# A hybrid trunk layer whose instruction order comes from the framework's timeline model instead of its functional simulator's clock

## The chip, the cores and the metric

The kernel runs on one core of one Trainium2 chip. A core has five engines with an instruction queue each: TensorE (PE; its weight loads are listed apart as PEld), VectorE (DVE), ScalarE (ACT), GpSimd (POOL) and SyncE (SP, which here only issues transfers). The metric is the device time of one execution in microseconds. Each engine takes its own instructions in the order in which they stand in its queue, and one that waits holds up all behind it.

## The reference

One layer of a decoder trunk, for one sequence of 512 tokens and a model width of 1024, in float32:

```python
h = rms_norm(x, norm1_g[i])
proj = h @ w_in[i]          # S5 input | q | k | v | RWKV-7 inputs | 3 groups of gates
y_a = s5_mixer(...)         # complex diagonal SSM, scan over time, GLU
y_b = diff_attention(...)   # 4 heads, QK norm, two softmaxes subtracted
y_c = rwkv7_mixer(...)      # 8 heads of 64: a state updated token by token
branch_out = jnp.einsum('blnc,ncd->blnd', branches, w_branch[i])
merged = jnp.sum(gates * branch_out, axis=2)
x = x + (merged @ w_out[i])
h2 = rms_norm(x, norm2_g[i])
gu = h2 @ w_ffn_in[i]
x = x + ((silu(gu[..., :D_FF]) * gu[..., D_FF:]) @ w_ffn_out[i])
```

Of the three mixers, the one that matters most below is RWKV-7's scan, in which each token's state needs the one before:

```python
sa = jnp.einsum('bhvk,bhk->bhv', state, a_t)
state = state * w_t + sa * b_t + v_t * k_t
y_t = jnp.einsum('bhvk,bhk->bhv', state, r_t)
```

## The kernel before

Activations lie transposed, 128 channels on the partitions and 512 tokens along the free axis. There are two kinds of work for TensorE.

**Dense matmuls.** Each projection (class `Dense`) keeps float32 accuracy with three reduced-precision matmuls for each block of 128 rows: high part times high part (L1296), high times low (L1297), low times high (L1298), 512 columns each. `tokens` (L1267 to L1285, for attention's k and v) does the same with 256 columns (L1280 to L1282). A weight block comes by a transfer, ScalarE makes its high part (L1225) and VectorE its low part (L1226). The dense matmuls of the mixers depend on nothing but `h` and their weights, so they can stand nearly anywhere.

**Small matmuls.** The mixers are long chains of small float32 matmuls, each of which TensorE does in two passes (an "x2" in the rows). RWKV-7 works on four pairs of heads, and each pair goes through these stages:

- prep (`_prep`, L360): two low-rank matmuls (L366, L371), and on VectorE the norm of `k` with a reciprocal root in a dozen tiny rows (`rsqrt`, L227 to L243; L239, L240 and L242 are its loop; L398 and L263 follow), whose sums are made by L258 and spread by L265; near its end VectorE's L421 writes `kb`.
- local (`_local`, L437): eight transposes of `kb` (L446), then the products within a chunk of 64 tokens (L464, L475).
- inverse (`_inverse`, L495): through DRAM and back (L503, L504), fifteen steps of two VectorE rows each (L513, L515), and through DRAM again (L522 to L527).
- join (`_join`, L535): six groups of small matmuls (L552 to L589), with a copy by ScalarE or VectorE between each and the next.
- chain (`chain`, L595): eight steps, one for each chunk. A step is L619 on TensorE (the state with this chunk's keys, `pT`), L621 on VectorE, L626 on TensorE (`pU`), L627 on ScalarE, then L631, L634 and L636 on TensorE, and L646 on VectorE, which makes the next state Z; ScalarE copies the outputs (L638) and scales Z (L650). L619 of the next step needs L646's Z.

S5's parameters, phases and quarters multiply complex tables on VectorE (`cmul`, L706 to L711) and have small matmuls of their own (L915, L931, L952, L963, L1001, L1005). Attention's are L1156, L1157, L1179 and L1184.

**What sets the order.** The program is written once, in the order that a string names (`ORDER`, line 43): P, T, I, J and C are prep, local, inverse, join and chain of the pair named by the digit, R the inputs of RWKV, S, H, U, Q and Y the pieces of S5, X, K and A those of attention, G one or more gates. The chains come as C0, C1, C3 and C2:

```python
ORDER = ("L R00 G1 R01 R02 P0 T0 I0 R10 R12 S R11 U0 P1 R20 R22 R21 T1 H0 G1 J0 U1 I1 J1 C0 P2 T2 F0 U3 U2 Q0 C1 G3 Q1 G2 H1 I2 Q2 R31 "
         "F1 R32 R30 P3 T3 J2 G1 I3 J3 C3 G1 Q3 X0 K0 A0 G2 Y0 C2 Y1 Y2 Y3 F3 X1 K1 G1 A1 F2 X2 K2 O0 O2 O3 G2 A2 X3 K3 G3 O1 A3")
```

This is not yet the order on the engines. The framework takes the whole program, walks it with a clock that says when each engine would be free and each operand ready, and lets instructions of later steps go ahead of those that are not ready; program order decides between several that are. The queues that come out of it are fixed when the kernel is built, and the chip only follows them. Buffers are chosen by the program before that, so a later user of a buffer waits for its readers in any order. After the mixers come the merge by gates, the output projection, SwiGLU (class `SevenProducts`) and the last projection, nearly all dense.

## Time and profile before

| | |
|---|---|
| median of 3 runs | 1011.51 us (1007.04 to 1014.56) |
| the profiled execution | 1011.71 us, its span 1009.9 us |
| mean granted clock of TensorE | 0.986 |
| busy: TensorE, VectorE, ScalarE, GpSimd | 968.3, 753.6, 473.2, 143.8 us |
| mixers | 0 to 537 us |
| merge, output projection, SwiGLU, last projection | 537 to 1009.9 us |

The page gives, for one execution, the busy time of each engine, the span in 40 slices, the transfers, the chain of work that ended last, and the costliest groups of instructions. The trace behind it gives the start and length of each instruction. A matmul's recorded length is from its start until its end leaves the pipeline, so two that follow each other overlap in the records. [...]

### The profile page before, as it was taken

What the parts mean: (1) busy time and instruction counts of PE and PEld (TensorE: products, weight loads), DVE (VectorE), ACT (ScalarE), POOL (GpSimd) and SP (SyncE); (2) the same over time, 40 slices, a digit from 0 to 9 for tenths busy, and PEclk for the clock granted to TensorE, in tenths of its full rate; (3) what the DMA queues carried; (4) which work ended last, traced back from release to release, by engine and by line L of the source; (5) the groups of instructions that cost most, each with busy time, mean ns of one, the idle gap of its engine ahead of it and who ended that gap; (6) DMA issues with size and microseconds to landing.
All of it is one profiled execution on the core that took longest, in us unless ns stands there. A gap on an engine that the chain in (4) does not pass through costs nothing. (4 is left out here: it accounts for less than half of the span.)

```text
span 1009.9 us, 17897 instructions
## 1 busy us (share of the span) xinstructions
PE 968.3 (96%) x6416; PEld 825.5 (82%) x6416; DVE 753.6 (75%) x1941; ACT 473.2 (47%) x978; POOL 143.8 (14%) x176
## 2 busy tenths in 40 slices
PE   6989999989999999999999899989999999999998
PEld 5767777767779787878886788889999999988886
DVE  7999666889996789977866555779989998843232
ACT  6634324424333566545455224556666666632220
POOL 3022020531420010000000332012211211000000
PEclk9999799999999999999999999989999999999999
DMA  7324252221333234252458864466667676344441
GB/s 242 116 75 112 66 121 75 74 55 53 101 106 75 79 95 126 84 157 74 152 166 282 241 206 151 143 153 159 152 160 183 143 153 169 73 149 122 136 131 37
DMA packets 105593, 129.95 MB, mean 129 GB/s; under 512 B 45376, under 2 KB 47296, under 8 KB 105504
## 3 DMA queue, kind: packets, MB, share of 16 engines
q1 hardware_dynamic: 99168, 117.28, 38.6%
q0 software_dynamic: 6336, 11.54, 7.4%
q8 instruction: 50, 0.82, 0.3%
q14 instruction: 39, 0.32, 0.1%
HBM read 109.90 MB, written 18.88 MB: 128 GB/s over the span
## 5 line engine op out<-in xcount | busy, mean ns | idle before, releaser
L1225 ACT CAST wh<-wr 128x512 fp32r<-128x512 f32 x198 | 120.3, 611 | 210.6 <-PE bank L1297 169.1
L1226 DVE TENSOR_TENSOR wl<-wr,wh 128x512 fp32r<-128x512 f32 x198 | 135.9, 689 | 81.1 <-ACT wh L1225 80.4
L1296 PE MATMUL bank<-act_hi,wh 128*128 128x512 f32 x360 | 149.3, 415 | 8.0 <-ACT wh L1225 5.9
L1297 PE MATMUL bank<-act_lo,wh 128*128 128x512 f32 x360 | 148.4, 412 | 2.0 <-DVE act_lo L253 2.0
L1298 PE MATMUL bank<-act_hi,wl 128*128 128x512 f32 x360 | 148.8, 413 | 0.0
L1385 PE MATMUL bank<-act_hi,wh 128*128 128x256 f32 x352 | 99.7, 283 | 3.4 <-ACT wh L249 3.4
L1385 PE MATMUL bank<-act_hi,wl 128*128 128x256 f32 x352 | 99.4, 283 | 0.2
L1385 PE MATMUL bank<-act_lo,wh 128*128 128x256 f32 x352 | 99.0, 282 | 0.0
L1385 PE MATMUL bank<-sp_t,wh 128*128 128x256 f32 x528 | 96.5, 283 | 0.0
L1296 PEld LDWEIGHTS bank<-act_hi,wh 128*128 128x128 f32 x360 | 69.6, 193 | 22.1 <-ACT wh L1225 5.9
L1297 PEld LDWEIGHTS bank<-act_lo,wh 128*128 128x128 f32 x360 | 69.4, 193 | 16.4 <-DVE act_lo L253 3.4
L1385 PEld LDWEIGHTS bank<-sp_t,wh 128*128 128x128 f32 x528 | 82.1, 191 | 0.0
L1298 PEld LDWEIGHTS bank<-act_hi,wl 128*128 128x128 f32 x360 | 69.4, 193 | 14.2 <-issue 0.6
L1385 PE MATMUL bank<-sp_t,wl 128*128 128x256 f32 x264 | 74.7, 283 | 0.0
L1385 PEld LDWEIGHTS bank<-act_hi,wh 128*128 128x128 f32 x352 | 67.7, 192 | 3.9 <-ACT wh L249 3.8
L1296 PE MATMUL bank<-act,wh 128*128 128x512 f32 x176 | 68.5, 389 | 0.0
L1297 PE MATMUL bank<-act,wh 128*128 128x512 f32 x176 | 68.5, 389 | 0.0
L1298 PE MATMUL bank<-act,wl 128*128 128x512 f32 x176 | 68.5, 389 | 0.0
L1385 PEld LDWEIGHTS bank<-act_hi,wl 128*128 128x128 f32 x352 | 67.4, 192 | 0.8 <-DVE wl L250 0.8
L1385 PEld LDWEIGHTS bank<-act_lo,wh 128*128 128x128 f32 x352 | 67.4, 192 | 0.0
L249 ACT CAST wh<-ar 128x512 fp32r<-128x512 f32 x79 | 48.2, 622 | 27.6 <-DMA ar<-in_w_ffn_in 13.3
L250 DVE TENSOR_TENSOR wl<-ar,wh 128x512 fp32r<-128x512 f32 x79 | 53.5, 687 | 9.1 <-ACT wh L249 7.0
(492 smaller groups left out, 2218.0 us busy)
## 6 DMA issues: line engine op xcount, KB each, us to landing
wr<-in_w_in SPq DMA_DIRECT2D x88, 256.0 KB, 3.0
ar<-in_w_ffn_in SPq DMA_DIRECT2D x46, 256.0 KB, 3.2
wr<-in_w_ffn_out SPq DMA_DIRECT2D x40, 256.0 KB, 2.7
gate<-ar SPq DMA_DIRECT2D x24, 256.0 KB, 2.5
wr<-in_w_branch SPq DMA_DIRECT2D x24, 256.0 KB, 3.3
ar<-gate SPq DMA_DIRECT2D x24, 256.0 KB, 3.4
ar<-in_w_ffn_in POOLq DMA_DIRECT2D x22, 256.0 KB, 3.9
sp_raw<-in_w_ffn_in SPq DMA_DIRECT2D x21, 256.0 KB, 3.2
```

Source lines behind the costliest of these rows:

```text
L249: nc.scalar.copy(hi, src)
L250: nc.vector.tensor_tensor(lo, src, hi.bitcast(F32), ALU.subtract)
L1225: nc.scalar.copy(wh, raw)
L1226: nc.vector.tensor_tensor(wl, raw, wh.bitcast(F32), ALU.subtract)
L1296: nc.tensor.matmul(ps, wh[:, j], hi(k), start=k == 0, stop=False)
L1297: nc.tensor.matmul(ps, wh[:, j], lo(k), start=False, stop=False)
L1298: nc.tensor.matmul(ps, wl[:, j], hi(k), start=False, stop=k == nk - 1)
L1385: nc.tensor.matmul(ps, w[x][:, c], b(y, j), start=first and j == js[0] and n == 0, stop=last and j == js[-1] and n == 2, skip_group_check= ...
```

## The change

```diff
@@ def kernel(**inputs) @@
-    with tile.TileContext(nc) as tc:
+    with tile.TileContext(nc, schedule_with_timeline_sim=True) as tc:
         trunk_kernel(tc, args, out)
```

The clock by which the framework walks the program is taken from another model: a timeline model of the engines in place of its functional simulator. The instructions stay the same, with the same operands and the same dependencies; their order in the queues differs. Of the 5542 matmuls of the kernel 3411 stand elsewhere in TensorE's queue, on VectorE 1691 of 1943 rows, on ScalarE 744 of 946, on GpSimd 88 of 180, and of SyncE's issues 294 of 474; nearly all of them belong to the mixers, and SwiGLU's order hardly changes. TensorE goes from dense to small matmuls or back 328 times in the order before and 198 times in the new one.

The first place is TensorE's queue in the chain of pair 3 (C3), about one and a half steps of it. Here `rw_T` is the tile `ts` that L621 writes and `rw_Z` the state Z. Before:

```order
L626 MATMUL bank_87<-rw_T_224,ar_9_77 128x128
L1296 MATMUL bank_83<-act_hi,wh_143 128x512
L1297 MATMUL bank_83<-act_lo,wh_143 128x512
L631 MATMUL bank_85<-ar_4_72,ar_1_69 128x128
L634 MATMUL bank_86<-ar_5_73,ar_4_72 128x128
L636 MATMUL bank_86<-ar_6_74,rw_Z_221 128x128
L1179 MATMUL bank_89<-ident,ar_6_74 128x128 x2
L1298 MATMUL bank_83<-act_hi,wl_144 128x512
L619 MATMUL bank_87<-rw_Z_222,ar_6_74 128x128
L1296 MATMUL bank_83<-act_hi,wh_148 128x512
```

And in the changed kernel:

```order
L626 MATMUL bank_87<-rw_T_224,ar_9_77 128x128
L631 MATMUL bank_85<-ar_4_72,ar_1_69 128x128
L634 MATMUL bank_86<-ar_5_73,ar_4_72 128x128
L636 MATMUL bank_86<-ar_6_74,rw_Z_221 128x128
L619 MATMUL bank_87<-rw_Z_222,ar_6_74 128x128
L626 MATMUL bank_85<-rw_T_223,ar_9_77 128x128
```

Attention's L1179 and the dense L1296 to L1298 no longer stand between the chain's matmuls. Counted over the whole queue (two matmuls of 256 columns as one of 512), 632 dense matmuls stand ahead of the first L446 of pair 3 before and 816 in the new order; from there to the fourth step of pair 2's chain the count rises to 807 before, and stays at 816 in the new order.

The second place is TensorE's queue at the end of the first chain (C0), where the prep of pair 2 (P2) begins: the last L619 and L626 of the chain, and the prep's L366 and L371. Before:

```order
L619 MATMUL bank_86<-rw_Z_221,ar_1_69 128x128
L1298 MATMUL bank_84<-act_hi,wl_140 128x512
L1296 MATMUL bank_84<-act_hi,wh_137 128x512
L1297 MATMUL bank_84<-act_lo,wh_137 128x512
L1298 MATMUL bank_84<-act_hi,wl_140 128x512
L626 MATMUL bank_87<-rw_T_224,ar_8_76 128x128
L366 MATMUL bank_86<-ar_10_78,rw_wl 128x512
L1296 MATMUL bank_84<-act_hi,wh_137 128x512
L634 MATMUL bank_85<-ar_3_71,ar_2_70 128x128
L636 MATMUL bank_85<-ar_1_69,rw_Z_221 128x128
L371 MATMUL bank_87<-ar_10_78,rw_wl 128x512
L1297 MATMUL bank_84<-act_lo,wh_137 128x512
```

And in the changed kernel:

```order
L619 MATMUL bank_86<-rw_Z_221,ar_1_69 128x128
L1005 MATMUL bank_89<-ar_12_80,ar_13_81 128x64 x2
L1001 MATMUL bank_89<-ar_6_74,ar_13_81 128x128
L1001 MATMUL bank_89<-ar_12_80,ar_14_82 128x128
L1005 MATMUL bank_89<-ar_12_80,ar_13_81 128x64 x2
L626 MATMUL bank_87<-rw_T_224,ar_8_76 128x128
L366 MATMUL bank_86<-ar_10_78,rw_wl 128x512
L634 MATMUL bank_85<-ar_3_71,ar_2_70 128x128
L636 MATMUL bank_85<-ar_1_69,rw_Z_221 128x128
L371 MATMUL bank_87<-ar_10_78,rw_wl 128x512
L915 MATMUL bank_90<-ident,ar_13_81 128x128 x4
L931 MATMUL bank_89<-ar_13_81,s5cb_s_1788 32x128 x4
```

Small matmuls of S5 stand where dense ones stood. From the fifth step of this chain to the first of the second (C1) four dense matmuls are left; the dense ones stand ahead of the fifth step (548 are ahead of it in the new order, 424 before) and in the second chain (744 ahead of its eighth step, 542 before).

The third place is VectorE's queue in the prep of pair 0 (P0), the end of the reciprocal root: L239, L240, L242 and L398 write its tiles `rqt_rw` and `ri_rw`, and the rows between them are `cmul` of S5. Before, with the small tables of S5's parameters:

```order
L239 TENSOR_TENSOR rqt_rw_487<-rqy_rw_494 128x8
L710 TENSOR_TENSOR s_tm_786<-s_pi_781,s_pr_780 128x16
L706 TENSOR_TENSOR s_pr_780<-s_pr_780 128x32
L240 TENSOR_TENSOR rqt_rw_487<-rqt_rw_487,rqx_rw_481 128x8
L711 TENSOR_TENSOR s_pi_781<-s_pi_781,s_tm_786 128x16
L806 TENSOR_TENSOR s_nr_823<-s_em_98_742,s_cth_774 128x16
L242 SCALAR_TENSOR_TENSOR ri_rw_480<-rqt_rw_487,rqy_rw_494 128x8
```

And in the changed kernel:

```order
L239 TENSOR_TENSOR rqt_rw_487<-rqy_rw_494 128x8
L710 TENSOR_TENSOR ar_12_80<-ar_12_80 128x8x8
L708 TENSOR_TENSOR ar_12_80<-ar_12_80 128x8x8
L240 TENSOR_TENSOR rqt_rw_487<-rqt_rw_487,rqx_rw_481 128x8
L711 TENSOR_TENSOR ar_12_80<-ar_12_80 128x8x8
L706 TENSOR_TENSOR ar_12_80<-ar_12_80 128x8x16
L242 SCALAR_TENSOR_TENSOR ri_rw_480<-rqt_rw_487,rqy_rw_494 128x8
```

The tiles in between are now those of the phases (H0), a step that stands thirteen steps behind this prep in `ORDER`: the parameters are done by then, and the table of phases, which stood behind this prep's L421 before, stands ahead of it.

## Rows read from the trace of the kernel before

**Rows 1.** The page: span and instructions; each engine's busy us, share and instructions.
```profile
span 1009.9 us, 17897 instructions
PE 968.3 (96%) x6416; PEld 825.5 (82%) x6416; DVE 753.6 (75%) x1941; ACT 473.2 (47%) x978; POOL 143.8 (14%) x176
```

**Rows 2.** Timeline of TensorE in the last projection: start, length, engine, line, operation.
```profile
899.75 0.39 PE L1298 MATMUL bank<-act,wl 128*128 128x512 f32 x1
899.98 0.39 PE L1296 MATMUL bank<-act,wh 128*128 128x512 f32 x1
```

**Rows 3.** Stretches: length; busy (instructions) by engine; granted clock, transfers' share, GB/s.
```profile
0.00:60.00 60.00, 47.41 (x204) 36.53 (x204) 51.80 (x198) 34.59 (x59) 15.52 (x45) 1.00 0.49 159
60.00:155.80 95.80, 93.42 (x730) 73.39 (x730) 70.88 (x217) 33.03 (x58) 14.80 (x18) 0.95 0.41 101
111.70:121.90 10.20, 10.20 (x44) 7.96 (x42) 3.28 (x6) 1.78 (x3) 0.00 (x0) 0.50 0.32 77
0.00:537.00 537.00, 507.66 (x3519) 408.69 (x3520) 436.63 (x1355) 251.65 (x548) 79.74 (x116) 0.98 0.37 107
537.00:1009.90 472.90, 460.68 (x2900) 416.77 (x2898) 316.94 (x588) 221.50 (x430) 64.02 (x60) 0.99 0.57 153
```

**Rows 4.** Timeline of one step of pair 1's chain on TensorE, 247.8 to 251.2 us.
```profile
247.78 0.41 PE L619 MATMUL bank<-rw_Z,ar 128*128 128x128 f32 x2
...
248.87 0.49 PE L626 MATMUL bank<-rw_T,ar 128*128 128x128 f32 x2
...
249.71 0.49 PE L631 MATMUL bank<-ar 128*128 128x128 f32 x2
...
250.04 0.39 PE L634 MATMUL bank<-ar,ar 128*128 128x128 f32 x2
...
250.26 0.39 PE L636 MATMUL bank<-ar,rw_Z 128*128 128x128 f32 x2
...
251.18 0.38 PE L619 MATMUL bank<-rw_Z,ar 128*128 128x128 f32 x2
```

**Rows 5.** Single lines: count, ns (least/median/most), first and last start; 289.9 to 383.
```profile
L446 PE MATMUL bank<-ident,kb_rw x8: 272/273/327, 289.9 to 291.6; 128*128 128x128 f32 x8
...
L589 PE MATMUL bank<-ar,ar x64: 191/191/212, 308.8 to 339.4; 32*32 32x32 f32 x64
...
L626 PEld LDWEIGHTS bank<-rw_T,ar x24: 186/189/192, 340.6 to 382.9; 128*128 128x128 f32 x24
```

**Rows 6.** Groups by line on TensorE, 289.9 to 382.8 us: busy us, mean ns | idle.
```profile
L1282 PE MATMUL bank<-wl,act_hi 128*128 128x256 f32 x58 | 16.8, 289 | 0.0
...
L1298 PE MATMUL bank<-act_hi,wl 128*128 128x512 f32 x30 | 12.8, 426 | 0.0
L1296 PE MATMUL bank<-act_hi,wh 128*128 128x512 f32 x29 | 12.2, 422 | 0.0
```

**Rows 7.** The same groups, 171.9 to 215.0 us.
```profile
L1297 PE MATMUL bank<-act_lo,wh 128*128 128x512 f32 x21 | 9.1, 432 | 0.0
```

**Rows 8.** Timeline of L626: fifth and eighth step of pair 0, first of pair 1.
```profile
171.92 0.38 PE L626 MATMUL bank<-rw_T,ar 128*128 128x128 f32 x2
...
186.09 0.63 PE L626 MATMUL bank<-rw_T,ar 128*128 128x128 f32 x2
...
214.99 0.38 PE L626 MATMUL bank<-rw_T,ar 128*128 128x128 f32 x2
```

**Rows 9.** Timeline of pair 0's first L446; in brackets its wait and releaser.
```profile
59.98 0.87 PE L446 MATMUL bank<-ident,kb_rw 128*128 128x128 f32 x6 [1.00 <-DVE kb_rw L421]
```

**Rows 10.** Groups by line on VectorE, 60 to 130 us.
```profile
L711 DVE TENSOR_TENSOR ar<-ar 128x8 f32<-128x8 f32 (+6 forms) x7 | 2.1, 298 | 0.0
L706 DVE TENSOR_TENSOR ar<-ar 128x8 f32<-128x8 f32 (+5 forms) x6 | 1.4, 234 | 0.0
```

**Rows 11.** Timeline of L634 in pair 1's chain, at a low and a full clock.
```profile
228.59 0.63 PE L634 MATMUL bank<-ar,ar 128*128 128x128 f32 x2
...
232.21 0.39 PE L634 MATMUL bank<-ar,ar 128*128 128x128 f32 x2
```

## The prediction

> **What bounds the kernel now.** I read the page first, then a table of stretches, then single stretches of the mixers. On the page TensorE is busy for 968 of 1009.9 us and VectorE for 754 [rows 1]. That busy figure hides what TensorE really does: a dense matmul is recorded as 0.39 us long, but the next one starts 0.23 us later [rows 2], so a TensorE that looks full can still be waiting between starts. I therefore count dense matmuls at 0.23 us each (512 columns) and half of that for 256 columns, and call the rest of a stretch its small matmuls and waits. The table of stretches [rows 3] splits the span in two: up to 537 us the mixers, where the idle time is 537 − 507.7 = 29.3 us, and from there 472.9 us of projections and SwiGLU with TensorE busy for 460.7. The order of the second part hardly changes, so I leave it as it is. VectorE is the second bound of the mixers, 436.6 us of 537.
>
> Inside the mixers the dense matmuls cover hops. One step of the RWKV chain goes from L619 over VectorE to L626, over ScalarE to L631, and over VectorE to the next L619: 1.09, 0.84 and 1.47 us, together 3.40 [rows 4]. TensorE's own part of it is five small matmuls of two passes, about 1.1 us at the 0.22 us between them; the dense matmuls fill the other two microseconds. The whole argument is about where that filling stands in the new order.
>
> **What the change removes, adds and moves.** No instruction's work changes; five orders do. Each moved dense matmul takes its time wherever it stands, if TensorE is the bound there. So a stretch that loses its filling costs the filling's time, less what the stretch itself becomes shorter.
>
> *The long bare stretch.* It begins with the first L446 of pair 3 (T3), goes over its inverse and join to its chain, and ends with the fourth step of pair 2's chain. Before, it lasts from 289.9 to 382.9 us, 93 us: 50.8 us up to the first L626 at 340.7, then eleven steps in 42.2, to the load of the twelfth L626 [rows 5]. In it stand 30 + 29 + 29 dense matmuls of 512 columns and 3 × 58 of 256 [rows 6] (of the lines left out there L1297 carries 29, L1280 and L1281 58 each): 88 × 0.23 + 174 × 0.115 = 40.2 us of filling. In the new order none is left there: 816 matmuls of 512 columns (two of 256 counted as one) stand ahead of it against 632 before, and 816 are still the count at its end. How short can it become? A bare chain step keeps its hops; of the 3.40 us about 0.2 was TensorE finishing a dense matmul, so I take 3.2 us, 35.2 for eleven. The part up to the chain is a serial walk too, and the join's groups L552 to L589 alone run until 339.4 [rows 5]; I take 46 us for it, 5 less than before, since fewer rows share its engines. So 81.2 us, 11.8 saved, and a **cost of 40.2 − 11.8 = +28.5**. Bounds: 40 if it gets no shorter, 17 if it saves twice that.
>
> *The short bare stretch.* From the fifth step of the first chain (171.92) over the eighth (186.09) to the first step of the second (214.99) there were 63 dense matmuls, 3 × 21, 14.5 us [rows 7, 8]. Now there are four, 0.9 us. The three steps took 14.2 us and may take 9.6. The 28.9 us behind them are one serial walk, prep and local of pair 2, and I keep them. **Cost 14.5 − 0.9 − 4.6 = +9**; bounds 4 (if the walk shrinks by 5) and 13.6.
>
> *The first prep.* L446 of pair 0 starts at 59.98 us and waits for VectorE's L421 [rows 9]. Now the rows of S5's phase table stand between the rows of this prep's rsqrt and ahead of L421: in L711, L706 and four sister lines the groups of small forms are 2.1 + 5 × 1.4 = 9.1 us [rows 10] (the sister lines are as L706), and about 6 us of splits and parameters come with them, 15 in all. VectorE was busy for 51.8 of the first 60 us [rows 3], so its 8 us of idle time can take some of it. I take **+12**; bounds 7 and 16. Who waits is TensorE: behind L446 in its queue stand the dense matmuls of the next tiles.
>
> *What is given back.* Between 60 and 155.8 us the new order puts 20 or so dense matmuls between the join's groups, where before there were three or four. The stretch has 2.4 us of idle time and 10.2 us at a granted clock of 0.50, which lose 5.1 us of work [rows 3]; I take **−8**, with bounds 0 and −15, as waits between starts don't show as idle time. In the second chain the steps have 20 or more dense matmuls in a hop now; TensorE stays the bound there, and that costs nothing beyond their own time.
>
> *The clock.* [...] At that level L634's two passes took 0.63 us against 0.39 [rows 11], 0.24 more; three hops a step make 0.7, and eleven steps 8, with some 5 for the join and local of pair 3: 13 us if all of it ran so. I take half, **+6**. [...]
>
> The sum: 28.5 + 9 + 12 − 8 + 6 = 47.5. The profiled execution took 1011.7 us (span 1009.9), the median of the runs is 1011.5, so both are one base: **1059 us**, with 1035 to 1085 as this case's own range.
>
> **The rivals.** *The longer dense runs pay for it all (not slower).* In the new order most hops outside the two stretches are covered by 20 matmuls instead of two to four, and TensorE alternates less often between dense and small. If all 29.3 us of the mixers' idle time and the 5.1 us of the slow clock came back, the late prep hid in VectorE's idle time and the clock stayed up, the sum would be 1011.7 + 28.5 + 9 − 34.4 = 1015. Against it: the idle time includes the start, before the first weights are there, and the waits of the same serial walks. The point that decides is the length of the long bare stretch: below 93 − 40 = 53 us it would cost nothing, and then the time would be near 990; eleven steps of 3.2 us alone take 35 of that, and the join's walk was never under 40.
>
> *Nothing gets shorter in the bare stretches, and the clock is low in them.* 40.2 + 13.6 + 16 + 13 with nothing given back is 82.8, or 1094 us. For it: the clock's row, and that VectorE's rows for attention stand in the long stretch too, so that its serial walk isn't alone. Against it: both chains' rows stand alone on VectorE in the new order, which makes steps shorter, not longer. It takes over where the long stretch stays near 93 us.
>
> *The moved rows are only prepaid.* Then 12 and 8 cancel more fully and the stretches save twice: 17 + 4 + 0 + 0 = 21, or 1033.
>
> **How the numbers follow.** Forecast (1035 to 1085): 0.62. Over 1085: 0.18. Between 1022 and 1035: 0.05. Within 1% of the median, which is about what a measurement of this kernel can tell from no change: 0.10. Faster by more: 0.05. So slower 0.85, same 0.10, faster 0.05. For 8 in 10 the range drops part of both ends: **1028 to 1096**.
>
> **What would show it.** In the profile after, the slices around 350 to 435 us should have low TensorE digits and a granted clock below full, with no L1296 to L1298 in some 80 us; L626 should follow L626 there by about 3.2 us. A second, shorter hole should lie near 220 to 255 us. The first L446 should start near 72 to 76 us instead of 60. The mixers should end near 584 us instead of 537, and the rest should again take about 473. If the long hole is under 60 us, or if dense matmuls stand in it, my main term is wrong; if the hole is there but the time is the same, the waits elsewhere were larger than the idle time shows; if L626 follows L626 by 4 us or more, VectorE's or ScalarE's rows or the clock set the step.

## The result and the profile after

| | before | after |
|---|---|---|
| median (lowest to highest) of 4 runs | 1013.03 us (1007.04 to 1019.71) | 1162.74 us (1161.87 to 1163.92) |
| ratio, 95% interval | | 1.1497 (1.1451 to 1.1542) |
| the profiled execution, its span | 1011.71, 1009.9 us | 1161.87, 1160.1 us |
| mean granted clock of TensorE | 0.986 | 0.903 |

The changed kernel is slower by 150 us. The forecast had the sign and said 47.5 us; 1163 lies far above its range. Some executions run slower, at a lower granted clock (1103.51 us at 0.926 in `new_to_T3`, whose other run took 1086.33 at 0.946); medians here and below are of all runs, while ratios and their intervals leave such runs out (two of the twelve of `measured3`, one of the two of `new_to_T3`). The granted clock is the PEclk of the page, TensorE's clock as a share of full speed; the traces of both kernels record it as 0.50 or 1.00, and a figure in between is a mean. The page after, in the form of [rows 1], with the slices of TensorE and of its granted clock:

```profile
span 1160.1 us, 17898 instructions
PE 1028.7 (89%) x6416; PEld 875.2 (75%) x6416; DVE 765.3 (66%) x1941; ACT 477.6 (41%) x978; POOL 135.6 (12%) x176
...
PE   7879989965899766799897868999899999999998
...
PEclk9889988975898875579998978999899999999999
```

VectorE and ScalarE do what they did. TensorE's recorded busy time grew by 60 us for the same matmuls, while its granted clock fell from 0.986 to 0.903, and its share fell from 96 to 89%. Every slice below 8 is among the first 24 (29 us each). The stretches after, with the columns of [rows 3]:

```profile
0.00:75.70 75.70, 55.91 (x239) 43.16 (x239) 68.33 (x269) 37.59 (x63) 20.64 (x51) 0.91 0.45 144
75.70:179.00 103.30, 97.54 (x766) 77.30 (x766) 63.85 (x156) 33.13 (x58) 10.43 (x14) 0.95 0.37 89
233.50:294.30 60.80, 38.09 (x277) 31.31 (x275) 39.62 (x87) 14.19 (x33) 13.02 (x16) 0.69 0.09 22
404.00:454.20 50.20, 33.26 (x446) 27.47 (x445) 34.00 (x131) 17.53 (x36) 3.81 (x3) 0.67 0.32 73
454.20:495.60 41.40, 31.30 (x102) 23.99 (x102) 10.58 (x42) 13.56 (x47) 0.00 (x0) 0.50 0.00 0
560.00:691.00 131.00, 109.09 (x507) 87.03 (x506) 78.69 (x214) 53.82 (x106) 0.00 (x0) 0.90 0.41 131
0.00:691.00 691.00, 575.09 (x3565) 467.10 (x3566) 456.97 (x1366) 259.36 (x557) 72.66 (x116) 0.85 0.31 90
691.00:1160.10 469.10, 453.66 (x2853) 408.07 (x2851) 308.37 (x576) 218.23 (x422) 62.99 (x60) 0.98 0.55 145
```

The mixers end at 691 us instead of 537, with 115.9 us of idle time instead of 29.3 and a clock of 0.85 instead of 0.98; what follows takes 469.1 us against 472.9. So the loss is made in the mixers, by their order.

Where it is made can be read from a few instructions that stand in both orders. For each I take its start in the two traces and the count of dense matmuls ahead of it in the queues. The lateness less 0.23 us for each dense matmul that is already done [rows 2] is the net loss up to there. (S5's small matmuls, of which some moved ahead too, aren't counted. Those from 179.0 to 233.5 us have recorded lengths of 21 us; if these overlap by about half, the rows in the middle are too high by up to some 10 us, an estimate.)

| instruction | before: start, dense ahead | after: start, dense ahead | late | prepaid | net |
|---|---|---|---|---|---|
| first L446 of pair 0 | 60.0, 161 | 75.7, 168 | 15.7 | 1.6 | 14 |
| first step of pair 0's chain | 155.8, 392 | 179.0, 432 | 23.2 | 9.2 | 14 |
| its fifth step | 171.9, 424 | 233.5, 548 | 61.6 | 28.5 | 33 |
| first step of pair 1's chain | 215.0, 486 | 294.3, 552 | 79.3 | 15.2 | 64 |
| its last step | 252.9, 542 | 365.7, 744 | 112.8 | 46.5 | 66 |
| first L446 of pair 3 | 289.9, 632 | 404.0, 816 | 114.1 | 42.3 | 72 |
| fourth step of pair 2's chain | 382.8, 807 | 495.6, 816 | 112.8 | 2.1 | 111 |
| its last step | 400.5, 848 | 540.1, 948 | 139.6 | 23.0 | 117 |
| last L1195, end of the mixers | 537.0, 1291 | 691.1, 1338 | 154.1 | 10.8 | 143 |
| end of the span | 1009.9 | 1160.1 | 150.2 | 0 | 150 |

The three largest parts are the two bare stretches (31 and 39 us) and attention's tail behind the last chain (27 us); then come the first chain (19) and the first prep (14).

### The profile page after: what moved, and what is told of

The parts are those of the page before. It is cut to its first block, busy times and chain, and to the rows that moved or that the text cites. A ratio compares the mean times of both kernels' runs of the same rounds, so it can differ in the third digit from the quotient of the medians.

```text
span 1160.1 us, 17898 instructions
## 1 busy us (share of the span) xinstructions
PE 1028.7 (89%) x6416; PEld 875.2 (75%) x6416; DVE 765.3 (66%) x1941; ACT 477.6 (41%) x978; POOL 135.6 (12%) x176
## 5 line engine op out<-in xcount | busy, mean ns | idle before, releaser
L1296 PE MATMUL bank<-act_hi,wh 128*128 128x512 f32 x360 | 152.2, 423 | 17.1 <-ACT wh L1225 6.1
L1298 PE MATMUL bank<-act_hi,wl 128*128 128x512 f32 x360 | 149.3, 415 | 0.0
L1296 PEld LDWEIGHTS bank<-act_hi,wh 128*128 128x128 f32 x360 | 71.7, 199 | 36.2 <-ACT wh L1225 6.1
L1298 PEld LDWEIGHTS bank<-act_hi,wl 128*128 128x128 f32 x360 | 70.9, 197 | 16.9 <-issue 0.2
L1296 PE MATMUL bank<-act,wh 128*128 128x512 f32 x176 | 68.5, 389 | 0.0
L1298 PE MATMUL bank<-act,wl 128*128 128x512 f32 x176 | 68.5, 389 | 0.0
```

What stands on the lines that cost most here:

```text
L1296: nc.tensor.matmul(ps, wh[:, j], hi(k), start=k == 0, stop=False)
L1298: nc.tensor.matmul(ps, wl[:, j], hi(k), start=False, stop=k == nk - 1)
```

## The experiments

All kernels here hold the queues by tables; three of them add matmuls. The changed kernel is written in the same program order, and order edges put each engine's instructions into the order of a table; such an edge adds no wait:

```diff
+def pin(tc, nc, ...):
+    """Orders each engine's queue as the tables say; order alone, no wait."""
+    ...
+        for a, b in zip(seq, seq[1:]):
+            tc.add_manual_dep(b, a.name, info, reason="pin")
@@ def kernel(**inputs) @@
         trunk_kernel(tc, args, out)
+        pin(tc, nc)
```

Apart from the added matmuls only the tables differ from kernel to kernel; the rest of this section says what stands in them. No run holds the changed order by a table and alters nothing; but where a table leaves a stretch alone the edges show no cost: pair 3's steps take 4.04 to 4.06 us in `dve_p2` as in the changed kernel.

### Dense matmuls alone put back, or moved alone

In `dense_back` the tables hold the new order, but each dense matmul of the mixers stands behind the small matmul of RWKV (of attention, after the last chain) behind which it stood before, and the other engines' rows that wait for a moved matmul go with it. Such a piece of TensorE's queue is

```diff
 L1297 MATMUL bank_84<-act_lo,wh_148 128x512
-L1298 MATMUL bank_84<-act_hi,wl_149 128x512
-L1296 MATMUL bank_84<-act_hi,wh_148 128x512
 ...
 L475 MATMUL bank_85<-ar_2_70,ar_3_71 64x64 x8
+L1298 MATMUL bank_84<-act_hi,wl_149 128x512
+L1296 MATMUL bank_84<-act_hi,wh_148 128x512
```

`dense_away` is its mirror: the order before, with the dense matmuls and the weight rows they need where the new one has them.

> Every queue is fixed. The order is that of the changed kernel, but each dense matmul of the mixers stands behind the same RWKV-7 row as in the kernel before (from the end of pair 2's chain on: behind the same RWKV-7 or attention row); VectorE's, ScalarE's and GpSimd's rows keep the new order, apart from those that wait for a moved matmul. Theory A, the dense matmuls were spent too early and the late hops stand bare: most of the 150 us comes back; what stays is the late first prep (14 us) and the slower walk through pair 2's prep (8 to 14 us), so 1030 to 1050 us, with the granted clock of the chains of pairs 3 and 2 back near 1.0. Rival B, the new order of VectorE's rows is what costs and the dense matmuls only fill time that is lost anyway: 1110 us or more.

> Every queue is fixed. The order is that of the kernel before, but the mixers' dense matmuls stand behind the same small matmuls as in the changed kernel (168, 432, 552, 816 and 816 of them ahead of pair 0's transposes, pair 0's chain, pair 2's transposes, pair 3's transposes and the fourth step of pair 2's chain), and the weight rows they need go ahead with them. Theory A: the two stretches stand bare here too, and the time rises by 43 us for the long one, some 18 for the short one and up to 27 in the tail: 1070 to 1110 us. Rival B: 1040 us or less.

Both were far off: 1439.01 us (1.4193, 1.4145 to 1.4242) and 1377.23 us (1.3591, 1.3552 to 1.3629). What TensorE waits for shows why, first in `dense_back`, then in `dense_away`, from 100 to 600 us (us in total, times, longest):

```profile
PE bank L1001 <- DVE ar L954: 19.1, 3, 7.5
...
PE bank L619 <- DVE rw_Z L646: 11.4, 5, 9.5
```

```profile
PE bank L1296 <- DVE ar L1592: 30.6, 5, 13.5
PE bank L552 <- DMA ar<-blocks: 24.6, 2, 13.9
```

L1592 is the gates' row that empties a dense matmul's bank: in `dense_away` moved matmuls stand at the head of TensorE's queue before their bank is free, and the chain waits behind them; in `dense_back` the small matmuls of S5 and of the chain wait for rows on VectorE, I take it since the dense matmuls now come ahead of what these rows need. An order of one kind of instruction means nothing without the order of the others that it was made with, so neither kernel weighs my term.

`y_back` moves less: only the dense matmuls that stand in the long stretch before, mostly attention's L1280 to L1282, go back there from the second chain.

```diff
 L619 MATMUL bank_85<-rw_Z_220,ar_4_72 128x128
-L1281 MATMUL bank_83<-wh_143,act_lo 128x256
-L1282 MATMUL bank_83<-wl_144,act_hi 128x256
 ...
 L626 MATMUL bank_86<-rw_T_223,ar_7_75 128x128
```

> Every queue is fixed. The order is that of the changed kernel, but the 262 dense matmuls that the kernel before has between pair 3's transposes and the fourth step of pair 2's chain (184 of 512 columns, two of 256 counted as one) stand there again, behind the same RWKV-7 rows; so they are missing between the third step of pair 1's chain and pair 3's transposes. Theory A: the long stretch takes no longer than bare (103 us from pair 3's first L446 to the fifth step of pair 2's chain), since there they fill waits, and the stretch they leave gets shorter by most of their 42 us, less the waits that then show in it: 20 to 35 us less in all, 1128 to 1143 us. Rival, they cost their own time wherever they stand: 1160 us again, the long stretch at 140 us.

It took 1246.83 us (1.2306, 1.226 to 1.2352), slower still. TensorE's waits from 370 to 600 us:

```profile
PE bank L1126 <- DVE ar L1123: 14.6, 2, 7.3
PE bank L1179 <- DVE ar L1175: 12.1, 5, 8.2
PE bank L552 <- DMA ar<-blocks: 8.8, 1, 8.8
```

The stretch from the second chain's fourth step to pair 3's transposes fell from 72.5 to 45.3 us, as expected, but the new order has attention's first head (L1126) ahead of pair 3's join, and its k and v come from the matmuls that I had moved; the join began 91 us after the end of pair 2's instead of 14. The miss is the same as in the two kernels above.

### The new order up to a place, the order before behind it

The rows that the kernel before starts ahead of a place come first, in the new order; all others follow in the order before. Both halves are whole, so no row waits for one that was moved away. The place is the prep of pair 2 (L366) in `new_to_P2`, the first L446 of pair 3 in `new_to_T3`, and the last step of pair 2's chain in `new_to_C2`:

```diff
 queues hold, for each engine:
-    every row in the new order
+    rows started before the place: in the new order
+    all others: in the order before
```

> Every queue is fixed. All rows that the kernel before starts ahead of pair 2's prep (1603 of 9069) come first, in the order of the changed kernel; the others follow in the order of the kernel before. So the same work stands on both sides of the cut as before, and no row waits behind a row of the other part. Theory A: the new order loses 14 us in the first prep, and more in pair 0's chain, where VectorE's rows of S5 now stand between the chain's own: the changed kernel reached this prep 65 us later with 114 more dense matmuls done (26 us at 0.23), so 39 us: about 1051 us. Rival, only the stretches without dense matmuls lose: 14 us, 1026.

> The same with the cut at pair 3's transposes (2495 rows first). The short bare stretch is in it, the long one is not. Theory A: the earlier run that took the dense matmuls of the long stretch away from this part reached pair 3's transposes at 372.8 us against 289.9 before, so 83 us more, 1095 us; the part behind the cut takes as long as before. Rival, the later part makes up for what the first loses, since it is the order of before with weights already there: 1060 or less.

> The same with the cut at the last step of pair 2's chain (3624 rows first): both bare stretches are in it, the tail with the last attention heads is not. Theory A: the changed kernel reached that step at 540 us with 964 dense matmuls done; with 848, as here, 27 us less, 513 against 400.5 before: 1125 us, so that the tail alone costs the other 37. Rival, the tail is only late and costs nothing of its own: 1150 or more.

They took 1047.33 us (1.0339, 1.0272 to 1.0406), 1086.33 us and 1136.87 us (1.1223, 1.115 to 1.1296). For `new_to_T3` I take the lower of two runs; the other took 1103.51 us, and the trace is of that one. There pair 3's first L446 is 72.3 us late, but its chain 89.0 us late. In between stands the order of before, with the same 98 dense matmuls (two of 256 columns as one); `new_to_T3` and then the kernel before:

```profile
362.20:429.80 67.60, 67.34 (x597) 56.74 (x598) 35.41 (x118) 19.80 (x41) 0.53 (x1) 0.70 0.20 46
```

```profile
289.90:340.70 50.80, 50.24 (x596) 42.45 (x597) 35.05 (x118) 19.74 (x40) 0.63 (x2) 1.00 0.25 61
```

The clock was 0.50 when the stretch began, behind a thinly filled end of the new order's part (the eight L446 start from 362.2 to 365.4 us, before from 289.9 to 291.6), and its mean of 0.70 makes some 40 of the 67.6 us at 0.50 (an estimate, with 1.00 for the rest), though TensorE was recorded busy for 67.34. These 16.8 us more are nearly the 17.2 us between the two runs.

Against 1013.05 us the three kernels are +34, +73 and +124, and the whole order has +150. So the stages cost 34, 39, 51 and 26 us (the 39 and 51 hang on one run; their sum doesn't), and in these kernels each loss stays lost: the expected sums held within 12 us, and no later row gave any of it back. My working gives 4, 9, 34.5 and 0 for the same stages.

In `new_to_P2` the last five steps of the first chain have nothing of other stages to fill them. Three of these steps:

```profile
198.40 0.80 PE L626 MATMUL bank<-rw_T,ar 128*128 128x128 f32 x2 [0.63 <-DVE rw_T L621]
...
202.45 0.80 PE L626 MATMUL bank<-rw_T,ar 128*128 128x128 f32 x2 [0.63 <-DVE rw_T L621]
...
218.68 0.80 PE L626 MATMUL bank<-rw_T,ar 128*128 128x128 f32 x2 [0.63 <-DVE rw_T L621]
```

A step is 4.05 us here, and five take 20.3, at a granted clock of 0.50. In the changed kernel this chain is filled, over-filled even, with work taken from the later stages: 120 dense matmuls from its first step to its last, where before there were 46. The loss is then met where that work is missing.

### The first prep alone

`late_prep` puts the rows that the new order starts ahead of pair 0's first L446 first, in the new order, and the order before behind them.

```diff
 queues hold, for each engine:
+    rows that the new order starts ahead of pair 0's first L446: in the new order
-    all others: in the new order
+    all others: in the order before
```

> Every queue is fixed. What the changed kernel starts ahead of pair 0's transposes comes first, in its order, with S5's table of phases in it; the rest follows in the order of the kernel before, which then finds that table done. Theory A: the 14 to 15 us by which the transposes start later are lost, as VectorE isn't the bound of what follows (70.9 us busy of 95.8): 1024 to 1030 us. Rival, the rows are only prepaid, and the stretch behind them gets shorter by what it no longer has to do: 1012 to 1018.

1019.26 us (1.009, 1.0054 to 1.0127), between the two expected ranges: some 7 us, of the 15.7 by which L446 is late there as well (75.7 us). By the first step of the first chain only 6.9 us of it are left, so that stretch got shorter by 8.8 us; VectorE finds S5's rows done there. With the new order behind it, 14 us stay.

### S5's rows out of pair 2's prep

In the second prep the rows of S5 stand between those of the reciprocal root. VectorE's timeline of the changed kernel (start, length, then the wait in brackets):

```profile
266.50 0.17 DVE L231 TENSOR_SCALAR rqx_rw<-bank 128x8 f32<-128x8 f32 x1 [3.38 <-PE bank L258]
...
267.33 0.69 DVE L970 TENSOR_TENSOR ar<-ar,bank 128x512 f32<-128x512 f32 x1 [0.46 <-PE bank L963]
...
272.26 0.84 DVE L994 TENSOR_TENSOR ar<-ar,ar 64x252 f32<-64x252 f32 x2
...
275.16 0.43 DVE L263 COPY ar<-ri_rw 128x512 f32<-128x512 f32 x1
```

and TensorE waits for its end and again for L421:

```profile
275.64 1.12 PE L265 MATMUL bank<-ident,ar 128*128 128x128 f32 x4 [8.42 <-DVE ar L263]
...
281.44 1.97 PE L446 MATMUL bank<-ident,kb_rw 128*128 128x128 f32 x8 [4.68 <-DVE kb_rw L421]
```

`dve_p2` moves these twelve rows of S5 (L970 to L994) behind pair 2's L466:

```diff
 L233 TENSOR_SCALAR rqi_rw_1595<-rqx_rw_1593 128x8
-L970 TENSOR_TENSOR ar_13_81<-ar_12_80,bank_89 128x512
-L971 TENSOR_TENSOR ar_14_82<-ar_12_80,bank_89 128x256
 L234 TENSOR_SCALAR rqi_rw_1595<-rqi_rw_1595 128x8
 ...
 L466 TENSOR_TENSOR ar_2_70<-bank_87,const 128x4x128
+L970 TENSOR_TENSOR ar_13_81<-ar_12_80,bank_89 128x512
+L971 TENSOR_TENSOR ar_14_82<-ar_12_80,bank_89 128x256
```

> Every queue is fixed as in the changed kernel, but the ten rows of S5 (L970 to L994, 7.2 us) that stand on VectorE between the rows of the reciprocal root in pair 2's prep go behind the last L466 of pair 2's local stage; no other engine's order changes but one row of GpSimd. Theory A: TensorE's wait of 8.4 us ahead of L265 falls to 1 or 2, and pair 2's transposes start 6 to 7 us earlier; the whole gets that much shorter, 1156 us. Rival, the rows are missed by whoever reads them, and the time stays at 1163.

```profile
270.53 1.11 PE L265 MATMUL bank<-ident,ar 128*128 128x128 f32 x4 [2.45 <-DVE ar L263]
...
276.31 1.97 PE L446 MATMUL bank<-ident,kb_rw 128*128 128x128 f32 x8 [4.66 <-DVE kb_rw L421]
```

L265's wait fell by 6 us and L446 came 5.1 us earlier, but the median is 1159.34 us (1157.56 to 1160.16), 3.4 us below 1162.74: the rows moved now stand ahead of the next prep's L231, for which an L626 waits 3.8 us. That is less than the 6 to 7 us expected. So these rows are worth about 5 us where they stand, and most of the short stretch's cost has other causes.

The trace shows where. From L366 to L231 the walk takes 15.1 us (251.4 to 266.5) against 6.2 before (186.4 to 192.6), from L231 to L263 8.7 against 3.7, and from there to the second chain 19.1 against 18.7. So the larger part, 8.9 us, lies ahead of the rows that `dve_p2` moved. VectorE's L375, the first row of the prep there, now waits behind wide rows of S5's `cmul`, and starts 4.7 us after L366 instead of 1.4; the changed kernel, then the kernel before:

```profile
254.52 1.61 DVE L710 TENSOR_TENSOR ar<-s_ri,ar 128x512 f32<-128x512 f32 x1
256.06 1.48 DVE L375 TENSOR_SCALAR ar<-ar 128x512 f32<-128x512 f32 x1
```

```profile
187.79 0.43 DVE L375 TENSOR_SCALAR ar<-ar 128x512 f32<-128x512 f32 x1 [0.71 <-ACT ar L368]
```

On TensorE L258, which L231 needs, stands behind S5's L952 and part of L963 (261.1 to 264.5); before, S5's matmuls of this walk came behind it. No run moved these rows.

### The clock of the bare chains

The changed kernel's chain of pair 3, a step of TensorE's timeline:

```profile
466.35 0.79 PE L626 MATMUL bank<-rw_T,ar 128*128 128x128 f32 x2 [0.65 <-DVE rw_T L621]
467.50 0.80 PE L631 MATMUL bank<-ar,ar 128*128 128x128 f32 x2 [0.35 <-ACT ar L627]
468.09 0.64 PE L634 MATMUL bank<-ar,ar 128*128 128x128 f32 x2
468.51 0.63 PE L636 MATMUL bank<-ar,rw_Z 128*128 128x128 f32 x2
468.97 0.79 PE L619 MATMUL bank<-rw_Z,ar 128*128 128x128 f32 x2
470.41 0.80 PE L626 MATMUL bank<-rw_T,ar 128*128 128x128 f32 x2 [0.65 <-DVE rw_T L621]
```

4.06 us, with L634 at 0.64 us, the length of the low clock in [rows 11]. Three kernels add dense matmuls, whose results nobody reads, to the bare chains of pairs 3 and 2. In `fill2` they are 384 columns wide, two behind each L619, L626 and L636, in the bank that this row has just written; `fill1` keeps only those behind L636. In `fill3` they are 512 columns wide, in a bank that nothing reads meanwhile, behind the same three rows in nine of the steps.

```diff
+    def fill(self, bank, c):
+        ...
+        for _ in range(FILL):
+            nc.tensor.matmul(bank[:, P:T], E.act_hi[:, 0, 0:P], E.act_hi[:, 1, 0:T - P], start=True, stop=True)
@@ def chain, behind L619, L626 and L636 (fill2); behind L636 (fill1) @@
+                    self.fill(py, c)
@@ fill3, behind L619, L626 and L636 @@
+        bank = E.pools["prw"].free[0]
+            nc.tensor.matmul(bank, E.act_hi[:, 0, 0:P], E.act_hi[:, 1], start=True, stop=True)
```

> Every queue is fixed as in the changed kernel, and work is added: behind L619, L626 and L636 of each step of pair 3's chain and of the first four steps of pair 2's, two dense matmuls of 384 columns into columns of the bank that nothing reads, 64 in all (at 0.23 us for 512 columns 0.17 us each, 11 us). Theory A, these steps are hops at a low clock with nothing in them: the added work costs nothing, the granted clock there goes from 0.50 to near 1.0, and the step of 4.04 us falls to 3.3 to 3.7; 2 to 8 us less than the changed kernel. Rival, TensorE is what bounds the step: 5.1 us a step and 11 us more. If the clock rises and the step stays at 4.0, the hops of VectorE and ScalarE set it, and my price for the clock was wrong.

> As fill2, with the added pairs of matmuls behind L636 alone, 21 of 2 x 384 columns less one for each first step: 40 in all were taken out behind L619 and L626, where VectorE and ScalarE waited for them (their readers came 0.35 us later in each of the two hops). Theory A: with two added matmuls a step the clock goes up as well, and the step, freed of twice 0.35 us, takes 3.83 - 0.7 = 3.1 us instead of 4.04: 10 us less than the changed kernel, 1152. If the clock stays at 0.50 with so few, the step stays near 4.0 and the time at 1163.

> As fill2, with bursts of two dense matmuls of 512 columns behind L619, L626 and L636 of nine steps (second to seventh of pair 3's chain, second to fourth of pair 2's), 54 in all (12.4 us at 0.23), now into a bank that no engine reads until the chain writes it again, so that no reader waits for them. Theory A: the clock goes to 1.0 in these steps and the hops are free of the 2 x 0.35 us that fill2 added: 3.83 - 0.7 = 3.1 us a step instead of 4.04, some 8 us less than the changed kernel in spite of 12.4 us of added work: 1153 to 1157. Rival, the low clock costs nothing on this path since VectorE and ScalarE set the hops: 4.0 us a step and 1163.

They took 1162.32, 1163.62 and 1151.38 us. The same stretch in `fill2`, `fill1` and `fill3` (columns as in [rows 3]; 0.50 in the changed kernel):

```profile
454.20:495.60 41.40, 31.56 (x160) 22.81 (x159) 10.36 (x41) 13.52 (x47) 0.00 (x0) 0.89 0.00 1
```

```profile
454.20:495.60 41.40, 31.99 (x108) 26.25 (x108) 9.95 (x38) 12.42 (x43) 0.00 (x0) 0.50 0.00 0
```

```profile
454.20:495.60 41.40, 35.39 (x173) 25.28 (x174) 14.80 (x52) 15.74 (x55) 0.00 (x0) 0.90 0.00 1
```

In `fill2` 64 added matmuls, some 11 us at the 0.23 us of [rows 2], brought the clock up from 0.50 to 0.89 and cost nothing in all (1162.32 us against 1162.74), but didn't give the 2 to 8 us that I expected. Its first two steps took 5.3 and 5.7 us, while the clock was still low (0.50 from 450 to 460 us, 0.82 from 460 to 470, 1.00 from there to 500), the next five 3.83 or 3.84 and not 3.3 to 3.7 (L638 is L626 here):

```profile
472.10 0.49 PE L638 MATMUL bank<-rw_T,ar 128*128 128x128 f32 x2 [0.65 <-DVE rw_T L633]
...
475.94 0.49 PE L638 MATMUL bank<-rw_T,ar 128*128 128x128 f32 x2 [0.65 <-DVE rw_T L633]
```

VectorE's L633 (L621) and ScalarE's L640 (L627) started only behind the fillers that follow their own matmul in the same bank; the trace names the filler as what they wait for, L640 for 19.5 us in 11 waits and L633 for 5.6 in four. `fill1` has 20 matmuls; the clock stayed at 0.50 and each pair only made the step longer, 4.51 us. (Of `fill2`'s 64 matmuls 44 are gone there, not the 40 of the expectation; of its two cases the one with a low clock came, with a longer step.) TensorE is recorded busy for 32.0 us of the 41.4 in `fill1`, at a clock of 0.50, and for 31.6 in `fill2`, at 0.89: the recorded busy time doesn't tell which clock was granted. `fill3` takes the sharing away (L639 is L626, L603 the filler):

```profile
469.69 0.49 PE L639 MATMUL bank<-rw_T,ar 128*128 128x128 f32 x2 [0.18 <-DVE rw_T L634]
469.94 0.71 PE L603 MATMUL bank<-act_hi 128*128 128x512 f32 x2
470.53 0.49 PE L645 MATMUL bank<-ar,ar 128*128 128x128 f32 x2
...
472.83 0.49 PE L639 MATMUL bank<-rw_T,ar 128*128 128x128 f32 x2 [0.18 <-DVE rw_T L634]
```

A step is 3.14 us, and the clock is 1.00 where these steps stand:

```profile
462.40:490.30 27.90, 24.04 (x132) 16.46 (x130) 8.99 (x36) 11.37 (x39) 0.00 (x0) 1.00 0.00 1
```

With 54 dense matmuls more, 12.4 us of work, the kernel is 11.4 us faster than the changed one, more than the 6 to 10 expected. In the trace it is 8.4 us ahead at the fifth step of pair 2's chain, with 3.1 of these from the step just behind the filled ones (8.6 us instead of 11.7); the rest comes behind the chains, where no matmul was added. So the clock of 0.50 cost 4.05 − 3.14 = 0.9 us in a bare step: the two passes of L619, L626 and L631, which end its three hops, take some 0.8 us each at 0.50 and 0.4 to 0.5 in `fill3` at 1.00. A step at 1.00 is 3.14 us there, the 3.2 of my working.

### Orders from measured durations

Does an order exist that beats both? I replayed the kernel with durations and hand-over times taken from the traces, chose queues by that replay, and fixed them by tables.

```diff
 queues hold, for each engine:
-    every row in the new order
+    every row in the order that the replay found shortest
```

`measured` takes program order between rows that are ready; `measured2` is the best of a search over priorities. Both replays let a row on VectorE overlap the end of the one before, also where it reads its result. In the rows of the changed kernel the first two are independent, the last two not:

```profile
268.26 0.17 DVE L234 TENSOR_SCALAR rqi_rw<-rqi_rw 128x8 int32<-128x8 int32 x1
268.34 0.17 DVE L236 TENSOR_SCALAR rqx_rw<-rqx_rw 128x8 f32<-128x8 f32 x1
...
274.29 0.17 DVE L239 TENSOR_TENSOR rqt_rw<-rqy_rw 128x8 f32<-128x8 f32 x1
274.49 0.17 DVE L240 TENSOR_TENSOR rqt_rw<-rqt_rw,rqx_rw 128x8 f32<-128x8 f32 x1
```

L236 starts 0.09 us ahead of L234's end, L240 0.03 us behind L239's. `measured3` and `measured4` are two searches with that mended, and TensorE's spacing taken by the kinds of both matmuls, the first from the start times in the trace of before, the second from program order.

> Every queue is fixed, in a third order: the same rule (of the rows that are ready, the first in program order), with a clock made of measured times: each row's own length in the eight traces so far, a dense matmul of 512 columns 0.23 us, and the measured hand-over from engine to engine (0.03 to 0.06 us behind the end of a row, a transfer as it landed). Replayed with these times, the eight orders run so far come out in the order in which the chip has them, 3.5 to 8% short: 972 for the kernel before, 1098 for the changed one. Theory A, what is wrong with the changed order is the length that its clock gives to hops and matmuls: the replay gives 951 here, which with the shortfall of the kernel before is 990 us; 662 dense matmuls stand ahead of pair 3's chain and 789 ahead of the fourth step of pair 2's, so neither stretch is bare. Rival, any clock of this kind comes out worse than the kernel before, because the granted clock or the transfers aren't in it: over 1020.

> As measured, but which of several ready rows goes first is found by trying: from a mix of program order and of the longest chain still ahead of a row, moved in small steps for as long as the replay got shorter, to 933. Theory A: 966 to 975 us. If the replay has been fitted to its own errors, no better than measured.

> An order found as measured2's was, with a mended clock: rows of VectorE that depend on the row ahead of them start 0.03 us behind its end and not 0.08 us ahead of it as independent ones do, and TensorE's time from one matmul to the next is taken by the kinds of both. It starts from the times that the kernel before had on the chip. Replayed, the kernel before is 999 (real span 1007), the changed kernel 1135 (1157), measured 1030 (1078), measured2 1002 (1040), and this order 958. Theory A, the clock was at fault: the replay falls short by 1 to 4%, so 970 to 1000 us, faster than the kernel before. Rival, the search finds the errors of any replay: 1015 or more.

> The same with program order as the starting point (so that it owes nothing to the order of the kernel before): replayed 960. Theory A: 970 to 1005 us. Rival: 1015 or more.

They took 1085.55 us (1.0703, 1.0665 to 1.0742), 1044.17 us (1.0303, 1.0267 to 1.0339), 1016.54 us (1.0031, 0.9994 to 1.0068) and 1023.03 us (1.0125, 1.0092 to 1.0157). None beats the kernel before, and all four came out above what the replay had promised. With the mended replay the search's result came down from 1044 to 1023 and 1017 us. (TensorE's time from one matmul to the next was also taken anew, and the searches differed in their starts, so how much of it is due to the one hand-over isn't shown.) What else the replay lacks, the granted clock perhaps, is open.

## Why the prediction was wrong in its size

| term | predicted | by the table of the result |
|---|---|---|
| first prep | +12 | +14 |
| given back between 60 and 155.8 us | −8 | 0 |
| first chain, steps one to four | 0 | +19, up to 10 of it S5's work done early |
| short bare stretch | +9 | +31 |
| second chain, and from there to pair 3 | 0 | +8 |
| long bare stretch, with the clock | +34.5 | +39 |
| rest of pair 2's chain | 0 | +6 |
| attention's tail | 0 | +27 |
| after the mixers | 0 | +7 |
| sum | +47.5 | about 150 |

**Right: the first prep.** The first L446 starts at 75.7 us, within the 72 to 76 that I gave, and waits for VectorE. (With the order before behind it, only 7 us of it are lost: `late_prep`.)

```profile
75.69 1.54 PE L446 MATMUL bank<-ident,kb_rw 128*128 128x128 f32 x6 [6.25 <-DVE kb_rw L421]
```

**Right in mechanism, near in size: the long bare stretch.** It has no dense matmul and a low clock (0.67 up to the chain, 0.50 in the chains), as I said. "11.8 saved" failed: it lasts 91.6 us against 92.9, so only 1.3 were saved. The part up to the chain took 50.2 us and not my 46, and the eleven steps 41.4 and not 35.2: within a chain a step is the 3.14 us of a full clock, my 3.2, plus the whole price of the low one, 0.9, where I took half of 0.7 (I had priced a hop by the 0.24 us that L634 loses in [rows 11], the longer one from a stretch at 0.50, 227.8 to 231.1 us; the matmuls that end the hops lose about 0.3). Of the eleven intervals only ten are steps; the one from pair 3's last step to pair 2's first is 0.6 us (0.3 before), so 35.2 was about 2.6 too much, and part of the nearness is luck. My sign "if L626 follows L626 by 4 us or more, VectorE's or ScalarE's rows or the clock set the step" came, and `fill3` says that it is the clock. The rival "Nothing gets shorter in the bare stretches, and the clock is low in them" describes it, and it takes over where I said that it would, near 93 us. My condition was right, the weight wrong. No row of before shows that the clock would fall in this stretch, which the +6 takes for granted: that was my estimate, and in place of the 6 the runs show 0.50 over its eleven steps and 0.9 us a step. In the changed kernel TensorE is recorded busy for 31.3 of the 41.4 us at 0.50, and `fill3`'s dense matmuls bring the clock up to 0.90 over the same time. But 0.50 isn't met with small matmuls alone: in the stretch from 111.7 to 121.9 us of before [rows 3] 17 of the 44 matmuls are dense, and at the spacing of 0.43 us that they had there these fill some 7 of its 10.2 us. What set the clock there isn't shown.

**Wrong: the short bare stretch.** The step that failed is "The 28.9 us behind them are one serial walk, prep and local of pair 2, and I keep them". From L366 of pair 2 to the second chain's first step it became 42.9 us. I asked only which dense matmuls leave this stretch, and took the walk's own rows to stand as before. The same small matmuls of S5 are in it in both orders (8 of L915 and L952, 16 of L931, 32 of L963), but they and S5's rows on VectorE now stand ahead of the prep's own: 8.9 us ahead of L231, 5.0 between L231 and L263. In the 42.9 us TensorE is busy for 24.2 at a clock of 0.63, where its small matmuls before took some 17 of 28.9 at 0.99 (28.7 busy, less 49 dense ones at 0.23, an estimate). The clock's share and that of the rows in the way overlap and were not taken apart by a run; `dve_p2` alone weighs one part, at about 5 us. The 31 us are then the lost filling, 14.5 − 0.9 = 13.6 as predicted, these 14, and 3.5 for the three steps ahead of the walk, which took 17.7 us (233.5 to 251.2) instead of 14.2, where I had expected 9.6.

**Wrong: "what is given back".** From 75.7 to 179.0 us, 103.3 against 95.8 with 33 dense matmuls more, 7.6 us: nothing came back. I take it that more filling didn't help hops that a few dense matmuls had covered already, as in the step of [rows 4]; that was not tested. The mean granted clock of the stretch is 0.95 in both: the 0.50 of 111.7 to 121.9 us is gone, but others stand at its ends (0.82 from 75 to 85 us, 0.50 from 165 to 170). And the idle time rose from 2.4 to 5.8 us.

**Missing: the first chain.** I put nothing on its steps one to four, which took 54.5 us instead of 16.1. Their 84 more dense matmuls make 19.3 of the 38.4 us, and S5's work done early up to some 10. TensorE waits for 2.9 us there, and its clock is 0.69 in the first 11; what else is in the rest is open.

**Missing: the tail.** I ended my count of dense matmuls at pair 2's chain and took the rest of the mixers as unchanged. But a filler can be used once. In the new order the chains of pairs 0 and 1 have 120 and 192 dense matmuls in their seven steps, where before 46 and 56 sufficed; 948 instead of 848 are gone at the end of the last chain, and attention's heads stand there with less around them. `new_to_C2` shows that the order of the tail costs 26 us; that the spent filling is why is read from these counts and the waits, and not tested. TensorE's waits from 560 to 691 us in the changed kernel:

```profile
PE bank L1179 <- DVE ar L1175: 6.5, 5, 3.6
PE bank L1156 <- ACT ar L1169: 5.6, 3, 2.0
```

and before from 413 to 537, where 122.16 of 124 us are busy:

```profile
PE bank L1195 <- DVE ar L1192: 0.8, 1, 0.8
```

Idle time is 21.9 us here against 1.8, and the clock 0.90 against 1.00. The same holds for the sentence "In the second chain the steps have 20 or more dense matmuls in a hop now; TensorE stays the bound there, and that costs nothing beyond their own time." It costs next to nothing there (+2); by this reading it is paid in the stretches behind.

**The range.** The wider one ends at 1096, near my second rival's sum of 1094. That had all of the known terms at their worst, but none for places that I had not looked at. 67 of the 102 us by which the forecast is short lie in such places (19, 8, 6, 27, 7). No run here tests that an order with fewer fillers in the first two chains would give those back within the new order: the kernels that moved them back alone brought waits of their own.

## What to carry to other kernels

Count the filling over the whole program, not only where it gets lost: dense work that over-covers one chain is missing in the next. So for each stage write down the start of a mark and the dense work ahead of it in both orders, and price every stage from mark to mark, also those that look unchanged. The bare chains here paid twice, for their filling (40.2 us in the long stretch) and for the clock (0.9 us of a step of 4.05 at 0.50). Dense work in their hops gave the clock back in two of three tries: `fill3`'s 54 matmuls brought it to 1.00 and the step to 3.14 us; `fill2`'s 64 to 1.00 too, but the step only to 3.83, as readers waited for them; `fill1`'s 20 left it at 0.50. When an order is tested by parts, cut it at a place in time for all engines together; moving one kind of row alone can leave it standing in a queue ahead of rows that don't wait for it.

## What had not been expected of the hardware

Adding 54 dense matmuls (12.4 us) to bare chains made the kernel 11.4 us faster, 8.4 of them by the end of the bare stretch and one step more: granted clock 0.90 instead of 0.50 from 454.2 to 495.6 us, steps of 3.14 us instead of 4.05. A thinner filler (20 matmuls, `fill1`) left the clock at 0.50 and made steps 4.51 us. In the changed kernel TensorE was recorded busy for three quarters of that stretch (31.3 of 41.4 us) with small matmuls alone, and the granted clock was 0.50 throughout. One and the same piece of queue took 50.8 us at a granted clock of 1.00 in the kernel before, and 67.6 us at 0.70 in a run of `new_to_T3` that entered it at 0.50. And on VectorE, in the changed kernel, L240, which reads the result of L239, started 0.03 us behind its end, where L236, independent of L234, started 0.09 us ahead of its end.
